# Recurrence projections in the mixer's first block, and transposes inside a block, in a hybrid encoder

## The chip, the cores and the metric

The kernel runs on one core of a Trainium2 chip. The metric is the device time of one execution in microseconds. The core has a matrix engine (TensorE, PE in the profile; its weight loads are PEld), a vector engine (VectorE, DVE), an activation engine (ScalarE, ACT), GpSimd (POOL) and a queue for loads (SyncE, SP).

## The reference

Two encoder layers over 256 tokens of width 1024, in float32. Each layer adds half a SwiGLU block, then a mixer, then half a SwiGLU block; a last norm follows.

```
x = x + 0.5 * swiglu(rms_norm(x, ffn1_norm), w_gate, w_up, w_down)
proj = rms_norm(x, mix_norm) @ w_in                     # 1024 -> 1792
xr, gate, q, k, v = split(proj, 512, 512, 512, 128, 128)
xc = depthwise_conv(xr, conv_w, width 4) + conv_b
r, i = sigmoid(xc @ w_a + b_a), sigmoid(xc @ w_x + b_x)  # 8 blocks, forward and backward
a = exp(-8 * softplus(-lam) * r); u = sqrt(1 - a*a) * (i * xc)
y_rec = gelu(gate) * (scan(a, u) + reverse scan(a', u'))
y_att = grouped attention(q, k, v, window, relative bias, sink)
x = x + concat(rms_norm(y_rec), rms_norm(y_att)) @ w_out
x = x + 0.5 * swiglu(rms_norm(x, ffn2_norm), ...)
```

## The kernel before

Tokens stand in two tiles of 128. Every product is made of three passes: activations and weights are each split into a high part (rounded) and a low part, and high x high, high x low and low x high are summed in PSUM. So each weight is loaded as raw float32 (`load_raw`, 1 MB pieces, three buffers, SyncE's queue), and `prep_one` makes a "half" of it: ScalarE copies the high part, VectorE subtracts it for the low part (for the halves in `VHI` VectorE does both). `prefetch` does that a few halves ahead; halves live in a ring of eight slots, except the mixer's first two, which use the tiles "w" and "i" (`EXTRA`).

There are eight PSUM banks in four pools of two: "a", "b", "g" and "c". `bank("gc")` takes "g" and "c" in turn, so that a bank comes back after four such allocations. "a" and "b" hold the output sums, the transposed tokens, and in the mixer attention's transposed probabilities ("b") and its output ("a").

The stages run one after the other. Between two of them stands `boundary` (L597): the stage before sums its last products (`tail`), residual updates, squares and norms of the two token tiles are put between them, `transposes(0)` turns the first tokens, and then `head(0)`, `transposes(1)` and `head(1)` of the stage that follows are issued. `transposes` (L534) makes eight transposes in TensorE and copies them into high (ScalarE) and low (VectorE) parts. TensorE, SyncE and GpSimd follow the order of the program; the order on ScalarE and VectorE is chosen by the planner when the kernel is built.

In a SwiGLU stage `head` (L699) multiplies one tile of tokens (stationary) by 512 columns, gate and up side by side: 3 passes of 8 matmuls. In the mixer `head` (L857) does so for the 256 columns of k and v only, both token tiles into one bank. The rest of the mixer follows a list, `ORDER` (L59). Each of its items is a letter and a number: x a recurrence projection (`xr`, L879: 24 matmuls of 256 columns, then the convolution `conv` on VectorE, read from PSUM), k the transposes of the keys (`head_end`, L872), q a query projection, l the gates of one quarter (`lru_gate`, L902: two banks, six matmuls each; ScalarE reads them with two activations a bank and makes two more), L the logits of two heads (two banks, read by VectorE, then exponentials on ScalarE), g a gate projection with its GELU, P, V and D the rest of attention, s a square root over all four quarters, c the scans, y their product with the gate, r, R, O and S the output projection.

Of the kernel before, what the change touches and what calls it, by code (L numbers as in the profile page):

```python
# [8 lines left out]
F32 = mybir.dt.float32  # L9
# [11 lines left out]
T = 256  # L21
# [34 lines left out]
CUT = 3  # L56
RCUT = 1
EARLY = 1
ORDER = "x0 k0 x1 q0 l0 q1 l1 L0 x2 L1 x3 g0 l2 P0 q2 l3 V0 P1 s0 L2 g1 c0 c1 q3 V1 P2 L3 c2 y0 g2 y1 V2 P3 g3 c3 V3 D0 y2 y3 r0 O0 r1 O1 r2 r3 R0 R1 R2 R3 S0".split()  # L59
HEAD = 2  # L60
VO = 6
VG = 1
# [5 lines left out]
def encoder_kernel(  # L68
# [56 lines left out]
    def bank(pool_):  # L125
        if pool_ == "gc":
            turn.append(turn.pop(0))
            pool_ = turn[0]
        return {"a": ps_a, "b": ps_b, "g": ps_g, "c": ps_c}[pool_].tile([128, 512], F32, tag=pool_, name="ps_" + pool_)
# [20 lines left out]
    def cols(w, c):  # L150
        return add_raw(w[:, c:c + 256].rearrange("(k p) c -> p k c", p=128), "kc")
# [7 lines left out]
    def head_half(name, r, j):  # L159
        add_half(name, [(r, j)], "kh")  # L160
# [26 lines left out]
        down(NM // 2 - 1)  # L187

    def plan_mix(st, wi, wo):
        r = cols(wi, 1536)  # L190
        for j in range(2):
            head_half((st, "kv", j), r, j)
        chunk = {}

        def chunk_of(n, p):
            if (n, p) not in chunk:
                chunk[n, p] = cols(wi, {"x": 0, "g": 512, "q": 1024}[n] + p * 256)
            return chunk[n, p]

        for n, i in ORDER:  # L200
            i = int(i)
            if n in "xg":
                col_half((st, {"x": "xr", "g": "gt"}[n], i), chunk_of(n, i // 2), i % 2)
            elif n == "q":
                add_half((st, "q", i), [(chunk_of("q", h), i * 64, h * 64, 64) for h in range(2)], "kc")
        for p in range(4):
            r = rows(wo, p * 256)
            for j in range(2):
                add_half((st, "o", 2 * p + j), [(r, j)], "rc")
# [118 lines left out]
    def W(*name):  # L328
        prefetch(index[name] + state["ahead"])
        return slot_t[name]  # L330
# [263 lines left out]
    def front():  # L594
        return tc.high_priority(offset=FRONT)

    def boundary(tail, evac, gi, head, ahead):  # L597
        prefetch(ahead)
        state["cap"] = ahead
        state["ahead"] = AHEAD  # L600
        tail(0, 0)
        with front():
            for hf in range(2):
                evac(0, hf)
                squares(0, hf)
            norm(0, gi)
        tail(1, 1)
        with front():
            evac(1, 0)
            transposes(0)  # L610
            squares(1, 0)
        tail(1, 2)
        with front():
            evac(1, 1)
            i1 = squares(1, 1)
            i2 = norm(1, gi)
        prefetch(ahead)
        state["behind"] = [i1, i2]
        state["cap"] = ahead + EARLY
        prefetch(ahead + FORCE)  # L620
        head(0)
        with front():
            state["behind"] = transposes(1)
        state["cap"] = 1 << 30
        prefetch(ahead + FORCE2)
        head(1)
        state["behind"] = []
        if gi % 3 != 1:
            load_gain(gi + 1)
# [61 lines left out]
    def ffn(st, acc_done):  # L691
# [4 lines left out]
        hn_t = {}  # L696
        late = {}

        def head(t):  # L699
            ps = bank("gc")  # L700
            ts_ = slice(t * 128, (t + 1) * 128)
            w = [W(st, "gu", q) for q in range(4)]
            for p in range(3):
                for k in range(KD):
                    x = cur["l" if p == 2 else "h"][:, k, ts_]
                    pe.matmul(ps, x, w[k // 2][p % 2][:, k % 2 * 512:k % 2 * 512 + 512],  # L706
                              start=(p == 0 and k == 0), stop=(p == 2 and k == KD - 1))
            hn_t[t] = gated(ps[:, 0:T], ps[:, T:2 * T])
            if t == 1:
                for q in range(4):  # L710
                    done((st, "gu", q))
# [126 lines left out]

    def mix(l):
        st = (l, 1)  # L840
        ps_x = {}
        xch_t, xcl_t = {}, {}
        xc_t, ge_t, a_t, yh_t, yl_t = {}, {}, {}, {}, {}
        q_t = mix_p.tile([128, NT, T], F32R, tag="q", name="q_t")
# [9 lines left out]
            done((st, name, i))  # L854
            return ps

        def head(t):  # L857
            if t == 0:
                ps_x["kv"] = bank("gc")
            ps = ps_x["kv"]  # L860
            natural([ps[:, t * 256:t * 256 + 256]], [[W(st, "kv", j) for j in range(2)]], t)
            if t == 1:
                for j in range(2):
                    done((st, "kv", j))
                new_tiles()
                act.activation(out=kv_t.rearrange("p t c -> p (t c)"), in_=ps, func=AF.Copy)

        def new_tiles():
            late["w"] = w_p.tile([128, 2 * NT, T], F32, tag="w", name="w_t")
            late["i"] = mix_p.tile([128, 2 * NT, T], F32, tag="i", name="i_t")  # L870

        def head_end():  # L872
            ps = bank("gc")
            for t in range(2):
                pe.transpose(ps[:, t * 128:(t + 1) * 128], kv_t[:, t, 0:128], eye_t)
            act.activation(out=k_t, in_=ps[:, 0:T], func=AF.Copy)
            dve.tensor_sub(out=kl_t, in0=ps[:, 0:T], in1=k_t.bitcast(F32))

        def xr(i):  # L879
            ps = unit("xr", i)  # L880
            with tc.high_priority(offset=MIXF):
                conv(i, ps)

# [333 lines left out]
```

## Time and profile before

| | |
|---|---|
| median of 3 runs | 938.35 us (937.91 to 938.55) |
| profiled execution | 938.13 us, of it span 936.4 us |
| PE busy | 926.0 us, 99% |
| PEld busy | 804.9 us, 86% |
| DVE busy | 696.8 us, 74% |
| ACT busy | 544.4 us, 58% |
| HBM read | 170.59 MB, 186 GB/s over the span |
| chain that ended last | PE 95%, DVE 2%, ACT 1%, issue 1%, DMA 1% |

Busy time of PE is modelled, since matmuls overlap: the distance from one start to the next tells the pace, and a gap between starts tells a wait. The shares are means over stages that are limited differently. The two mixers lie at about 197 to 286 us and 656 to 744 us; the granted clock is 1.00 in both.

### The profile page before, as it was taken

The numbers are of one execution on the slowest core, as the hardware profiler recorded it, in microseconds if no ns is written. First come the engines' busy times: TensorE is split into PE (matmuls) and PEld (weight loads), VectorE is DVE, ScalarE is ACT, GpSimd is POOL, SyncE is SP. The second block draws the span as 40 slices with busy tenths as digits, with TensorE's granted clock in tenths as the row PEclk, the third lists the DMA queues.
The fourth block names the chain that finished last, engine by engine and source line by source line (L and its number), as shares of the span: only waits on it lengthen the run. The fifth ranks groups of instructions, "written<-read, shape, count | busy, mean of one in ns | idle before, by whom it ended". The sixth has DMA issues, their size and how long they took to land.

```text
span 936.4 us, 13679 instructions
## 1 busy us (share of the span) xinstructions
PE 926.0 (99%) x5288; PEld 804.9 (86%) x5288; DVE 696.8 (74%) x1213; ACT 544.4 (58%) x1005; POOL 37.4 (4%) x60
## 2 busy tenths in 40 slices
PE   9999999999999999999999999999999999999997
PEld 8888888889988888888888888888999888888885
DVE  6888666769998876666688666666799887666663
ACT  7665555548855655555466555554687575555542
POOL 2300000000010000000030000000000100000000
PEclk9999999999999999999999999999999999999998
DMA  9786956714255755565557666555162576665521
GB/s 310 223 269 219 314 184 203 233 56 151 75 162 201 261 186 180 185 205 195 173 175 237 188 196 195 187 180 180 51 221 68 180 240 202 195 195 181 183 87 45
DMA packets 125009, 172.54 MB, mean 184 GB/s; under 512 B 3925, under 2 KB 108797, under 8 KB 124944
## 3 DMA queue, kind: packets, MB, share of 16 engines
q1 hardware_dynamic: 122192, 166.21, 54.8%
q0 software_dynamic: 2304, 4.87, 1.6%
q8 instruction: 41, 0.67, 0.3%
q10 hardware_dynamic: 448, 0.59, 0.2%
q14 instruction: 24, 0.20, 0.1%
HBM read 170.59 MB, written 3.16 MB: 186 GB/s over the span
## 4 chain that ended last, share of the span: by engine, by line
PE 95%; DVE 2%; ACT 1%; issue 1%; DMA 1%; POOL 0%; SPq 0%; POOLq 0%; DVEq 0%
PE ps_g L581 16%; PE ps_c L581 16%; PE ps_c L580 7%; PE ps_g L580 7%; PE ps_a L590 5%; PE ps_a L592 4%; PE ps_a L591 4%; PE ps_b L591 4%; PE ps_b L592 4%; PE ps_b L590 4%; PE ps_g L706 2%; PE ps_c L706 2%; PE ps_a L1021 1%; PE ps_g L569 1%; PE ps_g L570 1%; PE ps_g L571 1%
## 5 line engine op out<-in xcount | busy, mean ns | idle before, releaser
L308 DVE TENSOR_TENSOR wl<-raw,wh 128x1024 fp32r<-128x1024 f32 (+1 forms) x320 | 367.3, 1156 | 102.3 <-ACT wh L307 98.0
L307 ACT ACTIVATE wh<-raw 128x1024 fp32r<-128x1024 f32 (+1 forms) x306 | 301.9, 999 | 82.8 <-PE ps_b L592 60.5
L581 PE MATMUL ps_c<-xhl,wh 128*128 128x512 f32 x640 | 231.3, 396 | 0.0
L581 PE MATMUL ps_g<-xhl,wh 128*128 128x512 f32 x640 | 231.3, 396 | 0.0
L580 PE MATMUL ps_c<-xhl,wl 128*128 128x256 f32 x560 | 156.2, 279 | 0.0
L580 PE MATMUL ps_g<-xhl,wl 128*128 128x256 f32 x560 | 156.1, 279 | 0.0
L581 PEld LDWEIGHTS ps_c<-xhl,wh 128*128 128x128 f32 x640 | 120.1, 188 | 23.0
L581 PEld LDWEIGHTS ps_g<-xhl,wh 128*128 128x128 f32 x640 | 120.1, 188 | 23.0
L580 PEld LDWEIGHTS ps_c<-xhl,wl 128*128 128x128 f32 x560 | 105.6, 189 | 3.5
L580 PEld LDWEIGHTS ps_g<-xhl,wl 128*128 128x128 f32 x560 | 105.6, 188 | 3.5
L590 PE MATMUL ps_a<-wh,hh 128*128 128x512 f32 x168 | 65.7, 391 | 0.0
L590 PE MATMUL ps_b<-wh,hh 128*128 128x512 f32 x168 | 65.6, 391 | 0.0
L592 PE MATMUL ps_b<-wh,hl 128*128 128x512 f32 x168 | 65.4, 389 | 0.0
L591 PE MATMUL ps_b<-wl,hh 128*128 128x512 f32 x168 | 65.4, 389 | 0.0
L592 PE MATMUL ps_a<-wh,hl 128*128 128x512 f32 x168 | 65.4, 389 | 0.0
L591 PE MATMUL ps_a<-wl,hh 128*128 128x512 f32 x168 | 65.4, 389 | 0.0
L766 ACT ACTIVATE sg<-ps_g 128x256 f32<-128x256 f32 x40 | 15.4, 385 | 63.3 <-PE ps_g L581 63.3
L766 ACT ACTIVATE sg<-ps_c 128x256 f32<-128x256 f32 x40 | 15.3, 383 | 52.5 <-PE ps_c L581 51.6
L767 DVE TENSOR_TENSOR sg<-ps_g,sg 128x256 f32<-128x256 f32 x40 | 17.0, 425 | 32.8 <-ACT sg L766 32.7
L766 ACT ACTIVATE su<-ps_c 128x256 f32<-128x256 f32 x40 | 15.4, 386 | 39.0 <-PE ps_c L581 39.0
L754 ACT ACTIVATE hh<-th 128x256 fp32r<-128x256 f32 x80 | 33.4, 417 | 8.1 <-DVE th L748 7.8
L591 PEld LDWEIGHTS ps_a<-wl,hh 128*128 128x128 f32 x168 | 31.6, 188 | 6.9
(323 smaller groups left out, 1577.9 us busy)
## 6 DMA issues: line engine op xcount, KB each, us to landing
raw<-in_ffn_w_down_dram SPq DMA_DIRECT2D x44, 1024.0 KB, 5.0
raw<-in_ffn_w_gate_dram SPq DMA_DIRECT2D x43, 1024.0 KB, 5.4
raw<-in_ffn_w_up_dram SPq DMA_DIRECT2D x43, 1024.0 KB, 5.4
raw<-in_w_in_dram SPq DMA_DIRECT2D x14, 1024.0 KB, 5.5
raw<-in_w_out_dram SPq DMA_DIRECT2D x8, 1024.0 KB, 7.0
lb<-ld POOLq DMA_DIRECT2D x1, 2048.0 KB, 14.9
bias_t<-lb POOLq DMA_DIRECT2D x1, 1536.0 KB, 12.4
gain<-in_ffn_norm_dram SPq DMA_DIRECT2D x3, 512.0 KB, 4.6
```

The source lines that it names most:

```text
L307: act.activation(out=h3, in_=src, func=AF.Copy)
L308: dve.tensor_sub(out=l3, in0=src, in1=h3.bitcast(F32))
L569: pe.matmul(dst, wh[:, ks], xh[:, k, t0:t1], start=(k == 0), stop=False)
L580: pe.matmul(dst[:, 0:T], wl[:, ks], x2[:, 0, k, :], start=False, stop=False)
L581: pe.matmul(dst, wh[:, ks], x2[:, :, k, :], start=(k == 0), stop=(k == KD - 1))
L590: pe.matmul(acc[hf], ah[:, ts_], wh[:, cs], start=first, stop=False)
L591: pe.matmul(acc[hf], ah[:, ts_], wl[:, cs], start=False, stop=False)
L592: pe.matmul(acc[hf], al[:, ts_], wh[:, cs], start=False, stop=last)
L706: pe.matmul(ps, x, w[k // 2][p % 2][:, k % 2 * 512:k % 2 * 512 + 512], start=(p == 0 and k == 0), stop=(p == 2 and k == KD - 1))
L754: act.activation(out=hh, in_=src, func=AF.Copy)
L766: act.activation(out=s, in_=ps[:, T:2 * T], func=AF.Copy)
L767: dve.tensor_tensor(out=s, in0=ps[:, 0:T], in1=s, op=ALU.add)
```

## The change

The first block of the mixer gets the form of the SwiGLU stages' first block. Its four halves now hold k, v (256 columns) and the first two recurrence projections (256 columns) side by side; the first of them still use the tiles "w" and "i", the last two take the ring slots that the two projections' halves had. `head` makes 3 passes of 8 matmuls of 512 columns for each tile of tokens, into a bank of its own. ScalarE copies k and v of that tile into `kv_t`, and the 256 columns of the projections into `xn_x[t]`, in tiles that the SwiGLU stage uses. Since the block gives them with tokens on the partitions, `xr(0)` and `xr(1)` are no longer projections: two transposes each, into a bank of "a", from which the convolution reads. The transposes of the keys go to a bank of "b". In `boundary`, at all five boundaries, the second tokens' transposes and the prefetch behind them are issued within `head(0)`, ahead of its third pass. `ORDER` starts with q0, sets x2 behind q1, and moves l0, L1 and others accordingly.

```diff
--- before.py
+++ after.py
@@ -56,7 +56,7 @@
 CUT = 3
 RCUT = 1
 EARLY = 1
-ORDER = "x0 k0 x1 q0 l0 q1 l1 L0 x2 L1 x3 g0 l2 P0 q2 l3 V0 P1 s0 L2 g1 c0 c1 q3 V1 P2 L3 c2 y0 g2 y1 V2 P3 g3 c3 V3 D0 y2 y3 r0 O0 r1 O1 r2 r3 R0 R1 R2 R3 S0".split()
+ORDER = "q0 x0 k0 x1 q1 x2 l0 l1 L0 x3 L1 g0 l2 P0 q2 l3 V0 P1 s0 L2 g1 c0 c1 q3 V1 P2 L3 c2 y0 g2 y1 V2 P3 g3 c3 V3 D0 y2 y3 r0 O0 r1 O1 r2 r3 R0 R1 R2 R3 S0".split()
 HEAD = 2
 VO = 6
 VG = 1
@@ -187,10 +187,10 @@
         down(NM // 2 - 1)
 
     def plan_mix(st, wi, wo):
-        r = cols(wi, 1536)
-        for j in range(2):
-            head_half((st, "kv", j), r, j)
-        chunk = {}
+        chunk = {("x", 0): None}
+        r = cols(wi, 1536), cols(wi, 0)
+        for q in range(4):
+            add_half((st, "kv", q), [(r[0], q, 0), (r[1], q, 1)], "gu")
 
         def chunk_of(n, p):
             if (n, p) not in chunk:
@@ -199,6 +199,8 @@
 
         for n, i in ORDER:
             i = int(i)
+            if n == "x" and i < 2:
+                continue
             if n in "xg":
                 col_half((st, {"x": "xr", "g": "gt"}[n], i), chunk_of(n, i // 2), i % 2)
             elif n == "q":
@@ -618,11 +620,14 @@
         state["behind"] = [i1, i2]
         state["cap"] = ahead + EARLY
         prefetch(ahead + FORCE)
-        head(0)
-        with front():
-            state["behind"] = transposes(1)
-        state["cap"] = 1 << 30
-        prefetch(ahead + FORCE2)
+
+        def second():
+            with front():
+                state["behind"] = transposes(1)
+            state["cap"] = 1 << 30
+            prefetch(ahead + FORCE2)
+
+        head(0, second)
         head(1)
         state["behind"] = []
         if gi % 3 != 1:
@@ -696,11 +701,13 @@
         hn_t = {}
         late = {}
 
-        def head(t):
+        def head(t, between=None):
             ps = bank("gc")
             ts_ = slice(t * 128, (t + 1) * 128)
             w = [W(st, "gu", q) for q in range(4)]
             for p in range(3):
+                if p == 2 and between:
+                    between()
                 for k in range(KD):
                     x = cur["l" if p == 2 else "h"][:, k, ts_]
                     pe.matmul(ps, x, w[k // 2][p % 2][:, k % 2 * 512:k % 2 * 512 + 512],
@@ -838,7 +845,7 @@
 
     def mix(l):
         st = (l, 1)
-        ps_x = {}
+        ps_x, xn_x = {}, {}
         xch_t, xcl_t = {}, {}
         xc_t, ge_t, a_t, yh_t, yl_t = {}, {}, {}, {}, {}
         q_t = mix_p.tile([128, NT, T], F32R, tag="q", name="q_t")
@@ -854,30 +861,43 @@
             done((st, name, i))
             return ps
 
-        def head(t):
-            if t == 0:
-                ps_x["kv"] = bank("gc")
-            ps = ps_x["kv"]
-            natural([ps[:, t * 256:t * 256 + 256]], [[W(st, "kv", j) for j in range(2)]], t)
+        def head(t, between=None):
+            ps = bank("gc")
+            ts_ = slice(t * 128, (t + 1) * 128)
+            w = [W(st, "kv", q) for q in range(4)]
+            for p in range(3):
+                if p == 2 and between:
+                    between()
+                for k in range(KD):
+                    x = cur["l" if p == 2 else "h"][:, k, ts_]
+                    pe.matmul(ps, x, w[k // 2][p % 2][:, k % 2 * 512:k % 2 * 512 + 512],
+                              start=(p == 0 and k == 0), stop=(p == 2 and k == KD - 1))
+            act.activation(out=kv_t[:, t, :], in_=ps[:, 0:T], func=AF.Copy)
+            xn_x[t] = sum_p.tile([128, T], F32, tag=("sg", "su")[t], name="xn_x")
+            act.activation(out=xn_x[t], in_=ps[:, T:2 * T], func=AF.Copy)
             if t == 1:
-                for j in range(2):
-                    done((st, "kv", j))
+                for q in range(4):
+                    done((st, "kv", q))
                 new_tiles()
-                act.activation(out=kv_t.rearrange("p t c -> p (t c)"), in_=ps, func=AF.Copy)
 
         def new_tiles():
             late["w"] = w_p.tile([128, 2 * NT, T], F32, tag="w", name="w_t")
             late["i"] = mix_p.tile([128, 2 * NT, T], F32, tag="i", name="i_t")
 
         def head_end():
-            ps = bank("gc")
+            ps = bank("b")
             for t in range(2):
                 pe.transpose(ps[:, t * 128:(t + 1) * 128], kv_t[:, t, 0:128], eye_t)
             act.activation(out=k_t, in_=ps[:, 0:T], func=AF.Copy)
             dve.tensor_sub(out=kl_t, in0=ps[:, 0:T], in1=k_t.bitcast(F32))
 
         def xr(i):
-            ps = unit("xr", i)
+            if i < 2:
+                ps = bank("a")[:, 0:T]
+                for t in range(2):
+                    pe.transpose(ps[:, t * 128:(t + 1) * 128], xn_x[t][:, i * 128:(i + 1) * 128], eye_t)
+            else:
+                ps = unit("xr", i)
             with tc.high_priority(offset=MIXF):
                 conv(i, ps)
```

## Rows read from the trace of the kernel before

**Rows 1.** Windows, first mixer: stretch, us, busy of PE PEld DVE ACT POOL, clock, DMA

```profile
215.20:231.60 16.40, 16.36 (x140) 15.62 (x139) 15.69 (x41) 14.22 (x37) 0.00 (x0) 1.00 0.55 193
231.60:243.40 11.80, 11.80 (x106) 11.50 (x105) 11.61 (x23) 11.44 (x25) 0.00 (x0) 1.00 0.53 180
250.00:260.00 10.00, 10.00 (x87) 9.57 (x86) 10.00 (x33) 6.91 (x20) 0.00 (x0) 1.00 0.06 24
```

**Rows 2.** Timeline of TensorE, first mixer boundary: start, us, operation, count [idle before]

```profile
195.96 1.03 PE L544 MATMUL ps_a<-eye_t,xn 128*128 128x128 f32 x8
196.75 0.47 PE L590 MATMUL ps_b<-wh,hh 128*128 128x512 f32 x1
...
197.53 0.64 PE L561 MATMUL ps_c<-w_w,xhl 128*128 128x256 f32 x4
...
199.89 0.63 PE L561 MATMUL ps_c<-w_i,xhl 128*128 128x256 f32 x4
200.94 1.53 PE L544 MATMUL ps_b<-eye_t,xn 128*128 128x128 f32 x8 [0.42 <-DVE xn L526]
202.23 0.72 PE L561 MATMUL ps_c<-w_w,xhl 128*128 128x256 f32 x4
...
205.44 0.28 PE L569 MATMUL ps_g<-xhl,wh 128*128 128x256 f32 x1
```

**Rows 3.** Timeline of TensorE at the boundary between the two layers' SwiGLU blocks

```profile
471.18 1.98 PE L706 MATMUL ps_g<-wh,xhl 128*128 128x512 f32 x8
...
476.62 1.03 PE L544 MATMUL ps_b<-eye_t,xn 128*128 128x128 f32 x8
477.70 2.11 PE L706 MATMUL ps_c<-wh,xhl 128*128 128x512 f32 x8
...
481.46 1.98 PE L706 MATMUL ps_c<-wh,xhl 128*128 128x512 f32 x8
```

**Rows 4.** Timeline of VectorE: the second tokens' norm at those two boundaries

```profile
200.31 1.67 DVE L526 SCALAR_TENSOR_TENSOR xn<-x,rstd,gain 128x256 f32<-128x256 f32 x4 [0.66 <-POOL rstd L509]
...
473.96 1.67 DVE L526 SCALAR_TENSOR_TENSOR xn<-x,rstd,gain 128x256 f32<-128x256 f32 x4 [0.66 <-POOL rstd L509]
```

**Rows 5.** Timeline of TensorE, first mixer: gates l0, logits L1, gate projection

```profile
214.29 0.28 PE L911 MATMUL ps_g<-xch,gh_t 128*128 128x256 f32 x1
...
224.35 0.38 PE L976 MATMUL ps_g<-k_t,q_t 64*128 64x256 f32 x1
...
228.43 0.38 PE L569 MATMUL ps_c<-xhl,wh 128*128 128x256 f32 x1
```

**Rows 6.** Timeline of ScalarE: first and last operation of l0, first GELU square

```profile
215.21 0.48 ACT L919 ACTIVATE w_t<-ps_g,hba 128x256 f32<-128x256 f32 x1 [0.33 <-PE ps_g L913]
...
218.58 0.60 ACT L922 ACTIVATE w_t<-w_t,s_pos 128x256 f32<-128x256 f32 x1
...
231.61 0.39 ACT L940 ACTIVATE x<-ps_c 128x256 f32<-128x256 f32 x1 [0.25 <-PE ps_c L571]
```

**Rows 7.** Timeline of VectorE: first convolution begins, third begins and ends

```profile
208.52 0.55 DVE L888 TENSOR_SCALAR xc<-ps_g,par 128x256 f32<-128x256 f32 x1 [2.94 <-PE ps_g L571]
...
224.46 0.54 DVE L888 TENSOR_SCALAR xc<-ps_c,par 128x256 f32<-128x256 f32 x1
...
227.90 0.48 DVE L891 SCALAR_TENSOR_TENSOR xc<-ps_c,par,xc 128x255 f32<-128x255 f32 x1
```

**Rows 8.** Timeline of VectorE, then TensorE, at the fourth query and its logits

```profile
250.17 0.42 DVE L1116 SCALAR_TENSOR_TENSOR ql_t<-ps_g,q_t 128x256 fp32r<-128x256 f32 x1
250.64 0.38 PE L978 MATMUL ps_c<-k_t,ql_t 64*128 64x256 f32 x1
```

**Rows 9.** Timelines of SyncE's loads and of VectorE's residual update near the boundary

```profile
178.73 0.37 SPq L250 DMA_DIRECT2D raw<-in_w_in_dram  x1
183.13 0.37 SPq L250 DMA_DIRECT2D raw<-in_w_in_dram  x1
191.39 0.69 DVE L801 SCALAR_TENSOR_TENSOR x<-ps_a,x 128x512 f32<-128x512 f32 x1 [1.84 <-PE ps_a L592]
```

## The prediction

> **What bounds the kernel now.** I read the windows view over the attention block first, then the order of time of TensorE, ScalarE and VectorE, always asking which wait ends last there. In the mixer's attention block TensorE is busy without a break, and so, nearly, are VectorE and ScalarE [rows 1]: three engines share the bound, and VectorE is full for all of 250 to 260 us. That is what the reader should see: an edit that frees TensorE alone gains nothing further on unless the other two arrive earlier as well. At the change itself TensorE does wait. The first tokens' key/value block ends at 200.36, the second tokens' transposes wait for their normalised input and then the second block waits for the transposed copies: 202.23 before it goes on [rows 2]. The second layer repeats the pattern some 459 us later, so a net per mixer counts twice. The other three boundaries (before SwiGLU blocks) show less waiting [rows 3].
>
> **The change, part by part** (per mixer, first layer's clock).
>
> *Widening.* 48 key/value matmuls of 256 columns (20 in 2.36 us, 118 ns each [rows 2]) and the 48 of two recurrence projections (120 ns each: from 205.44 to 214.29 there are 72 such matmuls in 8.85 us, less 0.2 for two transposes [rows 2, 5]) become 48 of 512 columns at 227 ns (24 in 5.44 us [rows 3]). 5.66 + 5.76 - 10.88 = 0.5 us saved. A page of the Trainium skill speaks against even this: "TensorE: Matmul & The Clock Gate", section "Wait — 56ns, not 53.3ns?", gives a warm matmul its columns at 2.4 GHz and about 2.5 ns. By it 48 pairs would save an estimated 0.12 us, and the sum below would be 0.4 us worse per mixer. The trace differs, and its durations are used.
>
> *Added.* Four more 128x128 transposes, and all six now stand together: eight take 0.79 us [rows 2], so 0.6 + 0.1 for the change of kind, less 0.2 for the two that stood alone: 0.5 us lost. ScalarE gets four copies of 128x256 for one of 128x512, and eight weight pieces of 128x512 for four whole ones; VectorE the same pieces. These fall ahead of the convolutions, where VectorE waited 2.94 us for TensorE [rows 7] and ScalarE had as little to do; without that cover they would cost at most some 2 us of ScalarE, which joins the backlog below.
>
> *Moved transposes, mixer.* Before, 197.53 to 205.44 is 7.91 us for 5.66 of matmuls and 0.9 of transposes: 1.35 us of waiting [rows 2]. After, the transposes come up at 197.53 + 16 x 0.227 = 201.16. They cannot end before the second norm: it ends at 201.98 [rows 4], and TensorE went on 0.25 us behind it, so 202.23. That leaves 0.2 us of waiting; the eight matmuls behind (1.8 us) hide the copies of the transposed tokens. 1.1 us saved. What is queued behind the wait on TensorE is those eight matmuls; the prefetch (ScalarE, VectorE) that moves along is off the path.
>
> *Moved transposes, the other three boundaries.* Before: 471.18 to 483.27, 12.09 us [rows 3]. After: 3.63, then the transposes until 0.25 us behind the norm's end at 475.63 [rows 4], 475.88, then 0.1 + 1.8 + 5.4: 12.0 us. The wait for the copies is traded for a wait for the norm: 0 ± 0.1 us each.
>
> So TensorE alone would gain 0.5 - 0.5 + 1.1, about 1.15 us per mixer.
>
> *The new order.* Both gate blocks l0 and l1 now follow the third recurrence projection x2 without a projection between them, with logits L0 right behind. TensorE would reach l0 at 214.29 - 1.15 + 2 x 2.9 = 218.95. ScalarE's part of l0 begins 0.92 us after TensorE's [rows 5, 6], 219.87, and takes 3.6 us (215.21 to 219.1, less 0.3 of another operation [rows 6]). The four banks of the "gc" rotation return after four allocations. Counting through the new order, x3 reuses the first bank of l1, free only when ScalarE has done l0 and two operations of l1: 219.87 + 3.6 + 0.8 = 224.3 (0.5 less if an operation of l0 is passed over, 0.3 more if the copy of x2's convolution gets in between). By its own pace TensorE would be there at 223.2 (l0, l1 and L0 are the 10.06 us from 214.29 to 224.35 less two projections of 2.9 [rows 5]). So 0.6 to 1.4 of the 1.15 us is given back at once: the same work was done at 224.35 before. L1 moves behind x3.
>
> *ScalarE's backlog.* From 215.2 to 231.6 ScalarE did 14.22 us of work [rows 1], l0 first and the exponentials of L1 last; from 231.61 to the square root at 243.4 it works practically without idle time (11.44 of 11.8 us [rows 1, 6]). After, that work begins 4.66 us later. 0.6 us of it (a copy of q, one of a convolution) is done ahead, so it ends at 219.87 + 13.6 = 233.5 if nothing is left out, or at 231.6 if the two prefetch copies in it (1.9 us) are taken elsewhere. Against 231.6 that is 0 to 1.9 us late; I take one copy, 0.95 us, and give 0.55 back for the idle time that the chain had. The square root feeds the last scans, and behind it there is no room: the fourth query's low part ended at 250.59, and the matmul that reads it began at 250.64 [rows 8]. So I carry it through: **+0.4 us per mixer**, between -0.6 and +1.3. The lower end is a gain, since nothing excludes that both copies are out of the way.
>
> *Sum.* 938.13 (profiled execution, 936.4 span and 1.73 around it) + 2 x 0.4 + 3 x 0 = **938.9 us**. The profiled execution lies 0.2 us under the median of the runs, 938.35, with which it will be compared.
>
> **Rivals.** *TensorE's gain stays.* ScalarE fits its prefetch copies in while TensorE is at q1 and x2, where it has little to do, and works l1 off early. For it: two projections leave the rotation, so their convolutions hold no "gc" bank (before, the gate projection's start at 228.43 stands right behind the last step, at 228.38, of a convolution whose bank it takes [rows 5, 7]). Against it: [rows 1]. 938.13 - 2 x 1.15 = 935.8. A rule of the Trainium skill stands for this one: "Perfetto Trace Analysis", section "Matmul Optimizations", wants all eight PSUM banks used so that engines overlap, which here would mean that the convolutions read attention's idle banks while the rotation goes on.
>
> *The convolution holds l1's second bank, and the tail gets later.* x2's result now lies in the bank that l1's second half takes, four allocations on. Before, its convolution let go 4.1 us behind the matmuls (224.46 to 228.38, with other work in between [rows 7]); l1's second half wants the bank 2.2 us behind. If that spacing stays, TensorE stops for 1.9 us and ScalarE idles between as it did before (1.3 us). 0.95 + 1.3 - 0.25 = 2.0 us per mixer: 942.1. It decides from the point where x2's four convolution steps need over 2.2 us. For it: VectorE was never free there; against: its prefetch work can run ahead from 206 to 212 us, and then four bare steps take about 1.7 us.
>
> *A later load.* The split of the first chunk and the second chunk's now end together, so the second query chunk's load moves from 178.73 to about 183.13, when the next load's buffer came free [rows 9]. Four weight pieces behind it stand in ScalarE's and VectorE's order near the first tokens' residual updates. VectorE has 1.84 us of room there [rows 9], so 0 to 2.6 us per mixer reaches the first norm. At 1.2: 941.3.
>
> *The moved transposes do not do what they should.* If the norm came earlier by chance of the new order, all three other boundaries would save their 0.4 us: 937.7. If not, they save nothing, as in the sum.
>
> **How the numbers follow.** Forecast 0.46; gain stays 0.24; convolution holds the bank 0.18; later load 0.07; boundaries gain 0.05. The likeliest case alone spans 937.0 to 940.7 (-0.6 and +1.3 twice). To leave out no more than 2 in 10 the range goes from 935.7 to 942.0: half of the first rival lies about its lower end, and over a third of the second beyond its upper one. A measurement of this kernel can tell 0.2% from no change, about 1.9 us, so the borders are 936.5 and 940.2. Faster: most of the first rival and a trace of the forecast, 0.21. Slower: the second and third rival and the forecast's upper end, 0.29. Within: 0.50.
>
> **What would show it.** In the changed profile: 512-column matmuls of the mixer's first block at 227 ns and the second block starting without a gap (right); the first block's transposes at about 201.2 and their last pair waiting for the norm (right); TensorE waiting before x3, released by ScalarE's gate activations (right), or before l1's second half, released by a convolution step (second rival), or not at all with x3 at 223.2 (first rival). ScalarE should reach the square root 11.4 us behind the gate projection's square, 0.4 us later than before relative to the block's start. It is wrong if the two mixers differ from each other, if ScalarE is idle for over 2 us between l0 and the square root, or if the first norm of the mixer's boundary starts late.

## The result: 10.4 us slower, and the profile after

The changed kernel takes 948.71 us (median of 4 runs, 948.26 to 949.8) against 938.29 us (937.91 to 938.55): a ratio of 1.0112 (1.0100 to 1.0125). The forecast was 938.9 us, with 942.0 us as the upper end. The profiled execution took 948.88 us, its span is 947.1 us. TensorE's starts at the stage borders tell where the time went (us; the marks are the first transposes of a boundary, the transposes of a SwiGLU stage's first block's results, and the last matmul):

| stretch | before | after | longer by |
|---|---|---|---|
| start to the first mixer's boundary | 195.96 | 195.97 | 0.0 |
| first mixer | 195.96 to 284.47 | 195.97 to 289.65 | 5.2 |
| boundary behind it | to 303.73 | to 309.01 | 0.1 |
| SwiGLU stage | to 469.61 | to 474.92 | 0.0 |
| boundary between the layers | to 488.87 | to 494.16 | 0.0 |
| second layer's first SwiGLU stage | to 654.76 | to 661.68 | 1.6 |
| second mixer | to 743.26 | to 753.88 | 3.7 |
| boundary and last stage | to 929.11 | to 939.86 | 0.1 |

TensorE, first mixer, timeline of the changed kernel (answers to [rows 2] and [rows 5]):

```profile
197.54 0.63 PE L873 MATMUL ps_c<-w_w,xhl 128*128 128x512 f32 x2
...
201.25 1.23 PE L546 MATMUL ps_b<-eye_t,xn 128*128 128x128 f32 x8
202.24 0.71 PE L873 MATMUL ps_c<-w_w,xhl 128*128 128x512 f32 x2
...
209.71 0.28 PE L571 MATMUL ps_c<-xhl,wh 128*128 128x256 f32 x1
...
218.99 0.28 PE L931 MATMUL ps_g<-xch,gh_t 128*128 128x256 f32 x1
...
221.96 0.38 PE L931 MATMUL ps_g<-xch,gh_t 128*128 128x256 f32 x1 [1.37 <-ACT xch L919]
...
224.93 0.38 PE L996 MATMUL ps_c<-k_t,q_t 64*128 64x256 f32 x1 [0.38 <-DVE xc L911]
...
225.83 0.39 PE L571 MATMUL ps_g<-xhl,wh 128*128 128x256 f32 x1
...
229.82 0.39 PE L571 MATMUL ps_c<-xhl,wh 128*128 128x256 f32 x1
...
233.33 0.39 PE L931 MATMUL ps_g<-xch,gh_t 128*128 128x256 f32 x1 [0.38 <-DVE xc L911]
...
253.75 0.38 PE L998 MATMUL ps_c<-k_t,ql_t 64*128 64x256 f32 x1 [1.01 <-DVE ql_t L1136]
...
255.24 0.39 PE L571 MATMUL ps_c<-xhl,wh 128*128 128x256 f32 x1 [0.52 <-DVE ge L963]
```

Up to l0 at 218.99 everything is where the prediction had it (218.95). Then l1 (221.96) waits for its input, the second convolution; L0's second bank (224.93) and l2 (233.33) wait for the last step of a convolution, the third and the fourth; x3 starts at 225.83, the gate projection at 229.82. L3 waits at 253.75, and the gate projection behind it at 255.24.

VectorE, same kernel (answers to [rows 7] and [rows 8]), then ScalarE (answers to [rows 6]):

```profile
204.36 1.22 DVE L310 TENSOR_TENSOR wl<-raw,wh 128x1024 fp32r<-128x1024 f32 x1
210.88 0.69 DVE L307 CAST wh<-raw 128x1024 fp32r<-128x1024 f32 x1 [5.29 <-DMA raw<-in_w_in_dram]
211.61 2.43 DVE L310 TENSOR_TENSOR wl<-raw,wh 128x1024 fp32r<-128x1024 f32 x3
213.96 0.42 DVE L1136 SCALAR_TENSOR_TENSOR ql_t<-ps_c,q_t 128x256 fp32r<-128x256 f32 x1
214.29 0.54 DVE L908 TENSOR_SCALAR xc<-ps_a,par 128x256 f32<-128x256 f32 x1
...
218.64 0.55 DVE L908 TENSOR_SCALAR xc<-ps_a,par 128x256 f32<-128x256 f32 x1
...
253.28 0.42 DVE L1136 SCALAR_TENSOR_TENSOR ql_t<-ps_g,q_t 128x256 fp32r<-128x256 f32 x1
```

```profile
219.91 0.47 ACT L939 ACTIVATE w_t<-ps_g,hba 128x256 f32<-128x256 f32 x1 [1.66 <-PE ps_g L933]
...
221.49 0.42 ACT L919 ACTIVATE xch<-xc 128x256 fp32r<-128x256 f32 x1
...
246.10 1.92 ACT L1145 ACTIVATE w_t<-w_t 128x2048 f32<-128x2048 f32 x1
```

VectorE has nothing to do for 5.29 us ahead of 210.88 where it had 2.94 us [rows 7]: the planner put the cast of a gate weight first, and its load has not landed. Three subtractions of weights and a query's low part follow, so the first convolution begins at 214.29 (208.52 before) although its input was in PSUM at about 213.0, and the second one begins at 218.64. So of the 5.8 us by which the first convolution is later, some 4.5 us lie in when TensorE delivers its input, and 1.3 us in the work queued ahead of it. ScalarE's first gate activation comes at 219.91 (215.21), the square root at 246.10 (243.41).

The windows view from the second tokens' transposes to that square root (columns as in [rows 1]), of the changed kernel and then of the kernel before:

```profile
201.00:246.10 45.10, 42.89 (x328) 39.52 (x327) 37.97 (x88) 32.88 (x79) 0.00 (x0) 1.00 0.42 141
```

```profile
201.00:243.41 42.41, 42.32 (x356) 40.61 (x357) 38.41 (x84) 32.75 (x76) 0.00 (x0) 1.00 0.44 150
```

VectorE and ScalarE have the same work (38.0 and 38.4, 32.9 and 32.8 us). What grew is idle time: VectorE's from 4.00 to 7.13 us, ScalarE's from 9.66 to 12.22 us, TensorE's from 0.09 to 2.21 us. Of VectorE's 3.13 us, 2.35 stand ahead of the cast at 210.88.

Behind the square root nothing is made up. The chain of work that ended last (us from the start, duration, what ran) goes over VectorE alone until TensorE's gate projection:

```profile
248.56 1.20 DVE i_t L951 x2
249.76 0.60 DVE i_t L953
250.37 0.58 DVE i_t L955
...
253.36 0.33 DVE ql_t L1136
...
254.87 0.32 DVE ge L963
255.24 0.39 PE ps_c L571
```

The fourth query's low part is 3.11 us later than before (253.28 against 250.17 [rows 8]), and TensorE waits for it. The last step of the GELU (`ge`), whose end the gate projection waits for, begins at 254.79, 3.69 us later than in the kernel before, where one scan fewer stood ahead of it on VectorE:

```profile
251.10 0.40 DVE L943 SCALAR_TENSOR_TENSOR ge<-x,ps_c 128x256 f32<-128x256 f32 x1
```

Then, in the first mixer only, the granted clock falls (windows view, first and second mixer):

```profile
252.20:255.20 3.00, 1.51 (x13) 1.06 (x12) 3.00 (x8) 1.22 (x3) 0.00 (x0) 1.00 0.00 0
255.20:259.40 4.20, 4.16 (x22) 4.16 (x23) 4.20 (x16) 2.48 (x9) 0.00 (x0) 0.59 0.02 6
717.95:720.95 3.00, 1.48 (x13) 1.06 (x12) 3.00 (x8) 1.20 (x3) 0.00 (x0) 1.00 0.00 0
720.95:725.15 4.20, 4.18 (x36) 4.18 (x36) 4.20 (x16) 2.97 (x11) 0.00 (x0) 1.00 0.02 4
```

Both mixers have the same wait; after the first one TensorE got 22 matmuls done in 4.2 us, after the second one 36. That is the difference between 5.2 and 3.7 us.

The other place that lost time is the second layer's first SwiGLU stage. ScalarE, then TensorE, timelines of the changed kernel:

```profile
489.24 0.63 ACT L380 ACTIVATE gh_t<-gw 128x512 fp32r<-128x512 f32 x1 [2.94 <-DMA gw<-in_lru_w_x_dram]
...
496.16 1.06 ACT L309 ACTIVATE wh<-raw 128x1024 fp32r<-128x1024 f32 x1 [1.43 <-DMA raw<-in_ffn_w_down_dram]
497.13 0.36 ACT L773 ACTIVATE su<-ps_c 128x256 f32<-128x256 f32 x1
```

```profile
504.52 0.47 PE L583 MATMUL ps_g<-xhl,wh 128*128 128x512 f32 x1 [1.37 <-DVE hl L762]
```

ScalarE's queue has copies that wait for loads (2.94 and 1.43 us) ahead of the stage's first sums, and TensorE waits 1.37 us in the end, for a low part from VectorE.

### The profile page after: what moved, and what is told of

Its sections match the earlier page's. It is cut to its first block, busy times and chain, and to the rows that moved or that the text cites. A ratio compares the mean times of both kernels' runs of the same rounds, so it can differ in the third digit from the quotient of the medians.

```text
span 947.1 us, 13528 instructions
## 1 busy us (share of the span) xinstructions
PE 929.0 (98%) x5200; PEld 802.6 (85%) x5200; DVE 695.7 (73%) x1221; ACT 545.8 (58%) x1019; POOL 37.5 (4%) x60
## 4 chain that ended last, share of the span: by engine, by line
PE 89%; DVE 5%; issue 2%; ACT 1%; DMA 1%; POOL 1%; POOLq 0%; DVEq 0%; ACTq 0%
PE ps_g L583 15%; PE ps_c L583 15%; PE ps_g L582 7%; PE ps_c L582 7%; PE ps_a L592 4%; PE ps_a L594 4%; PE ps_a L593 4%; PE ps_b L594 4%; PE ps_b L593 4%; PE ps_b L592 4%; PE ps_c L873 1%; PE ps_g L873 1%; PE ps_c L713 1%; PE ps_g L713 1%; PE ps_a L1041 1%
## 5 line engine op out<-in xcount | busy, mean ns | idle before, releaser
L774 DVE TENSOR_TENSOR sg<-ps_g,sg 128x256 f32<-128x256 f32 x40 | 17.0, 425 | 32.8 <-ACT sg L773 32.7
```

The source lines that it names most:

```text
L774: dve.tensor_tensor(out=s, in0=ps[:, 0:T], in1=s, op=ALU.add)
```

## The experiments

Theories in turn: **A**, the loss lies in the mixer's new order, where VectorE's cast and subtractions ahead of the convolutions hold l1. **R**, the prediction's own: ScalarE's backlog holds the banks. **S**, the start of ScalarE's gate work sets the square root. **V**, VectorE's time lost ahead of its first convolution is not made up. For the SwiGLU stage (FFN in the expectations): **B** and **G2**, the moved transposes put weight copies ahead of the stage's first sums in ScalarE's queue; **G**, the split of the gate weights, which waits for its load there, does so by itself. "Mixer loss" is the lengthening between the marks of the table, first and second mixer; "(clock)" says that the granted clock fell in it.

**The move alone** (e1_move): the kernel before with the move at all five boundaries, in the mixer's old, narrow block too (cut):

```diff
-        head(0)
-        with front():
-            state["behind"] = transposes(1)
...
+        head(0, second)
```

> The kernel before with one part of the change alone: the second tokens' transposes issued ahead of the last third of the first tokens' block at all five boundaries; the mixer keeps its narrow first block and its old order. Theory A (the loss sits in the mixer's new order): the move by itself gives what the prediction's step on the moved transposes took, 1.1 us in each mixer and nothing at the three other boundaries, 938.1 - 2.2 = 935.9 us. Theory B (the loss of 1.76 us in the FFN behind the fourth boundary comes from the move, through ScalarE's changed order): 935.9 + 1.8 = 937.7 us.

Measured: 945.12 us, 1.0075 (1.006 to 1.009). Both theories fall. In the narrow block the transposes wait for the norm wherever they stand (1.35 us at 200.99), and the third pass now comes behind them: x0 starts at 206.11, 0.67 us later than before. The first mixer loses 2.6 us, 1.9 of it up to the first transposes of probabilities; TensorE waits 1.07 us at 230.34 for a convolution. The second mixer loses 1.5 us. The SwiGLU stage loses 3.6 us, its wait followed by a lower clock.

**The wide block and the order alone** (e2_widen):

```diff
-        head(0, second)
+        head(0)
+        second()
```

> The changed kernel without the moved transposes: the wide first block and the new order alone, the second tokens' transposes behind the whole first block as before. Theory A (l1 waits because VectorE has a cast that waits for its load, and three subtractions, queued ahead of the first convolution): in this kernel's order the three subtractions stand behind that convolution, and TensorE comes to l0 some 1.1 us later, so l1's wait of 1.65 us goes and with it most of what follows: 938 to 942 us. Theory R (the prediction's own: ScalarE's backlog behind the four gate steps in a row holds the banks): the order on TensorE is the same, so the loss stays and 1.1 us for each mixer comes on top: 948.7 + 2.2 = 951 us.

Measured: 948.86 us, 1.0118 (1.0101 to 1.0135); mixer loss 5.3 and 5.4 us (clock in both), nothing in the SwiGLU stage. q0 starts at 209.94, with the move at 209.71: the move is worth 0.23 us. l1 still waits (1.00 us), so A does not hold in this form; R had 951 us, more than was lost.

**Weight work held behind the second convolution** (e3_hold; `late["conv"]` is that convolution's last step; cut):

```diff
+                if n + i == "x1":
+                    state["behind"] = [late["conv"]]
+                if n + i == "l1":
+                    state["behind"] = []
```

> The changed kernel with one edit: the weight work that is queued from x1 to l1 is ordered on VectorE behind the second convolution's last step, so that no cast waits for its load ahead of the convolutions. TensorE's order and all its work stay. Theory A (VectorE's order): l1's wait of 1.65 us goes in both mixers, and the later waits that follow from it shrink: between 948.7 - 3.3 = 945.4 and 948.7 - 7.4 = 941.3 us. Theory R (ScalarE's backlog): l1's start moves, its successors wait for the banks as long as before: 948 to 949 us.

Measured: 948.06 us, 1.0105 (1.009 to 1.012). VectorE of this kernel, timeline:

```profile
212.68 0.54 DVE L908 TENSOR_SCALAR xc<-ps_a,par 128x256 f32<-128x256 f32 x1 [7.44 <-PE ps_a L898]
```

The cast is gone from ahead of the convolution, which begins 1.3 us earlier (this run stands 0.34 us ahead from its start on), and of l1's wait for it 0.55 us are left, for the low part. But VectorE now idles 7.44 us, and TensorE has other waits: 0.39 us at l1 for ScalarE, 1.33 us at L0's second bank for x2's convolution; mixer loss 4.2 us in both (clock in both). The fall of the clock is part of the 4.2 us, and how large a part is not known here; the loss without it may be under 3.7 us. The wait for the load is not the whole cause.

**L0 ahead of l1** (e4_L0first):

```diff
-ORDER = "q0 x0 k0 x1 q1 x2 l0 l1 L0 x3 ...
+ORDER = "q0 x0 k0 x1 q1 x2 l0 L0 l1 x3 ...
```

> The changed kernel with L0 ahead of l1 in the mixer's order, nothing else. Theory A (l1 waits for the second convolution, which is late on VectorE): L0, some 1.5 us of TensorE's work that needs only q0 and k0, covers most of l1's 1.65 us: 948.7 - 2.6 = 946.1 us; what comes later (VectorE's late chain) stays. Theory R (ScalarE's backlog): l1's gate work now comes still later on ScalarE, nothing is won: 948.7 us or up to 1 us more.

Measured: 952.87 us, 1.0152 (1.0137 to 1.0167), worse than either theory had it: mixer loss 7.2 and 6.3 us (clock in both). In the second mixer L0's second bank waits 1.67 us for ScalarE, the fourth query 1.42 us for VectorE.

**The old order** (e5_oldorder):

```diff
-ORDER = "q0 x0 k0 x1 q1 x2 l0 l1 L0 x3 L1 g0 ...
+ORDER = "x0 k0 x1 q0 l0 q1 l1 L0 x2 L1 x3 g0 ...
```

> The changed kernel with the order of the kernel before (x0 k0 x1 q0 l0 q1 l1 L0 x2 L1 x3 ...): the wide first block and the moved transposes stay, and l0 comes one and a half projections earlier. Theory S (the gate work of ScalarE and VectorE, 26 to 28 us from the first gate activation to the square root in either kernel and nearly without gaps, is what the mixer waits for; the change lets it begin at 219.9 where it began at 215.2): the first gate activation comes at 215.5 to 216.5, and the mixer's loss shrinks from 5.2 and 3.7 us to 1 us or less each; with the 1.8 us in the second layer's first FFN left, 939 to 943 us. Theory A alone (VectorE's cast ahead of the convolutions is the cause, wherever l0 stands): the cast is still ahead, 946 us or more.

Measured: 946.78 us, 1.009 (1.0073 to 1.0107); mixer loss 3.0 and 4.4 us (clock in the second). The cast, waiting for its load, still stands first on VectorE, the first convolution begins at 211.6, the first gate activation comes at 217.42 and the square root at 245.72, 28.3 us behind it (28.2 before). S had the distance right and the start wrong. The time is the one that A had (946 us or more), but the first convolution's input was in PSUM at about 211.0, so the cast held it for some 0.6 us only.

**x2 between l0 and l1** (e6_x2between), on top of the held weight work:

```diff
-ORDER = "q0 x0 k0 x1 q1 x2 l0 l1 L0 x3 ...
+ORDER = "q0 x0 k0 x1 q1 l0 x2 l1 L0 x3 ...
```

> The kernel of the run with the held weight work, with x2 moved from ahead of l0 to between l0 and l1, nothing else. Theory S (when the gate work begins decides): the first gate activation moves from 219.6 to 216.7, and as much as 2.9 us of each mixer comes back, less what the stretch has to spare: 948.1 - 4 to 6 = 942 to 944 us. Rival (the banks: four gate and logit steps bunched on TensorE wait for ScalarE's reads in any order): under 1 us in each mixer, 946 to 948 us.

Measured: 950.47 us, 1.0136 (1.0121 to 1.0151). Counted from the same start, the first gate activation does come earlier (217.38 instead of 219.92), the square root does not (248.99 instead of 247.46): S falls as the sole rule. Mixer loss 6.2 and 6.4 us (clock in both). L0's second bank waits 2.74 us for ScalarE.

**Gate-weight splits later** (e7_split, three steps of the stage later in the program, second layer; cut):

```diff
-                if st[1] == 0 and GSPLIT <= m < GSPLIT + 4:
+                if st[1] == 0 and GSPLIT + 3 * st[0] <= m < GSPLIT + 4 + 3 * st[0]:
```

> The changed kernel with the second layer's gate-weight splits three steps of the FFN later, nothing else. Theory G (TensorE's wait of 1.5 us at 502.8 comes from ScalarE, which has a gate-weight split queued ahead of the FFN's weight work and waits 2.9 us there for that split's load): the wait at 502.8 goes, 948.7 - 1.7 = 947.0 us. Rival (the FFN's own loads are late there, the split only fills the time): the wait stays, 948.7 us.

Measured: 948.79 us, 1.011 (1.0095 to 1.0125). It did not do what it was for: the planner left the split where it was, ScalarE waits 3.39 us for it at 488.67. The stage loses 1.3 us. Its mixers lose 3.7 and 3.7 us, without a fall of the clock.

**Old order, held weight work, later splits** (e8_oldhold, the edits of e5_oldorder, e3_hold and e7_split together):

> The changed kernel with three edits: the old order, the weight work held on VectorE behind the second convolution, and the second layer's gate-weight splits three steps later. Theory S with G: the first gate activation at about 214.5 (215.2 before the change), no wait in the second layer's first FFN, so no loss against the kernel before and up to 0.7 us won in each mixer: 937 to 939 us. If 941 us or more, a further loss is not yet named.

Measured: 957.99 us, 1.0212 (1.0196 to 1.0227), the slowest of all; mixer loss 8.2 and 7.4 us. The first gate activation comes at 215.43, as before the change, the square root at 245.59. The weight work that was held back (VectorE 32.7 us busy up to the square root instead of 38.0) comes later instead: the fourth query's low part lets TensorE wait 1.90 us, and stretches behind it wait for VectorE too.

**Splits queued 100 us later** (e9_gates, second layer; cut):

```diff
+                        if st[0] == 1:
+                            behind.enter_context(tc.issue_after(late["hh"].ins))
+                        split_gates(st[0], *divmod(m - GSPLIT, 2))
```

> The changed kernel with the second layer's four gate-weight splits queued on ScalarE behind the activations of the FFN's steps 12 to 15, some 100 us later; the earlier try moved them in the program but not in ScalarE's queue. Theory G (ScalarE's wait of 2.9 us for the gate weights' load, ahead of the FFN's weight work, makes TensorE wait 1.5 us at 502.8): that wait goes, 948.7 - 1.7 = 947.0 us. Rival (the FFN's own loads are late there): the wait stays, 948.7 us.

Measured: 949.18 us, 1.0111 (1.0094 to 1.0128). The splits are gone from ScalarE there, and the stage still loses 1.0 us; the mixers lose 5.2 us each (clock in both). ScalarE of this kernel:

```profile
496.38 1.06 ACT L309 ACTIVATE wh<-raw 128x1024 fp32r<-128x1024 f32 x1 [2.73 <-DMA raw<-in_ffn_w_down_dram]
497.35 0.36 ACT L773 ACTIVATE su<-ps_c 128x256 f32<-128x256 f32 x1
```

and of the kernel without the move (e2_widen), at the same place:

```profile
494.37 0.38 ACT L774 ACTIVATE su<-ps_c 128x256 f32<-128x256 f32 x1 [0.57 <-PE ps_c L583]
...
495.78 2.01 ACT L309 ACTIVATE wh<-raw 128x1024 fp32r<-128x1024 f32 x2 [0.72 <-DMA raw<-in_ffn_w_down_dram]
```

With the move a weight copy that waits for its load stands ahead of the stage's sum; without it, behind. The split is one such copy, not the only one.

**Less VectorE work, and its control** (e10_conv on the changed kernel, e11_convb on the kernel before): three of four convolution steps left out (cut).

```diff
             dve.tensor_scalar(o, ps, w(2), b, ALU.mult, ALU.add)
-            for j, d, n in ((0, 2, T - 2), (1, 1, T - 1)):
...
-            dve.scalar_tensor_tensor(out=o[:, 0:T - 1], in0=ps[:, 1:T], scalar=w(3), in1=o[:, 0:T - 1],
...
```

> The changed kernel with three of the four steps of each convolution left out (its output is not the reference's): some 4.9 us less VectorE work in each mixer, ahead of the square root; TensorE's and ScalarE's work as it was. Theory V (the wide block leaves VectorE without work for 5.3 us where it had 2.9 us without, in a stretch in which it is 90% busy and can't make that up): the mixers' loss of 5.2 and 3.7 us goes for the most part, 948.7 - 6 to 9 = 940 to 943 us. Theory S (ScalarE, 24.9 us of work from 219.9 to the square root): the square root stays where it is, 947 us or more.

> The kernel before with the same three steps of each convolution left out, as the control. All theories: TensorE is busy without gaps there (42.32 of 42.41 us up to the square root), so VectorE's 4.9 us less win next to nothing: 937 to 938.5 us. If it is 936 us or less, VectorE already held the kernel before in other places.

Measured: 942.50 us, 1.0052 (1.0031 to 1.0073), and 939.14 us, 1.001 (1.000 to 1.0019). The control gains nothing, as foreseen (it even loses 0.4 us per mixer, with a wait of 0.88 us for the fourth query). The changed kernel gains 6.2 us. Windows view of e10_conv, up to its square root:

```profile
201.00:244.05 43.05, 42.23 (x328) 39.39 (x327) 34.22 (x77) 32.60 (x79) 0.00 (x0) 1.00 0.43 148
```

TensorE idles 0.82 us there instead of 2.21, and the first mixer loses 1.2 us (the second 2.7, clock). The profiled execution took 946.1 us; its SwiGLU stage lost 3.8 us (clock). Its first convolution still begins late, at 214.23: less work on VectorE gives most of the first mixer's loss back. Shorter convolutions also bring l1's input sooner, so this alone does not separate VectorE's load from one late result; e3_hold, where that result came earlier and TensorE waited at L0's second bank instead, speaks for the load without proving it.

**Less ScalarE work** (e12_act): exponential and second tanh of both directions in one instruction each (cut; the exponential, the tanh likewise).

```diff
-                act.activation(out=a, in_=w, func=AF.Exp, scale=s_neg[:, c, pc:pc + 1], bias=s_neg[:, c, pc:pc + 1])
...
+            act.activation(out=a_t[c], in_=w2, func=AF.Exp, scale=s_neg[:, c, pc:pc + 1], bias=s_neg[:, c, pc:pc + 1])
```

> The changed kernel with the last two gate activations of both directions done by one instruction each, with the first direction's constants (its output is not the reference's): some 0.55 us less ScalarE work for each of a mixer's four gates, 2.2 us in a mixer. Theory S (ScalarE's work from the first gate activation sets the square root): 2 us come back in each mixer, 948.7 - 4 = 944.5 us. Theory V (VectorE's lost time): 947.5 to 949 us.

Measured: 946.84 us, 1.0101 (1.008 to 1.0123), between the two. The second mixer loses 2.2 us instead of 3.7, the first one 4.6 (clock, behind a wait of 1.95 us at l1, which the second has too). ScalarE is part of the bound as well; how the loss divides between the two engines stays open, since the planner lays out both queues anew with every edit.

**The lateness alone** (e13_qfirst), in the kernel before:

```diff
-ORDER = "x0 k0 x1 q0 l0 q1 l1 ...
+ORDER = "q0 x0 k0 x1 l0 q1 l1 ...
```

> The kernel before with q0 ahead of x0, k0 and x1 in the mixer's order, nothing else: the same TensorE work, l0 in the same place, only the first convolution comes one projection (2.9 us) later to VectorE. Theory V (VectorE's time lost ahead of its first convolution is not made up): a loss of 2 to 3 us in each mixer, as in the changed kernel with the old order, where the first convolution began equally late: 942 to 944.5 us. Rival (the loss needs the wide block; here only l0 can wait, 1 us or less): 938.2 to 940.2 us.

Measured: 946.54 us, 1.0091 (1.0074 to 1.0108): more than V had, 4.3 and 3.9 us per mixer (clock in the first). VectorE, timeline, and the windows up to the square root in the first and second mixer:

```profile
208.96 0.42 DVE L1116 SCALAR_TENSOR_TENSOR ql_t<-ps_g,q_t 128x256 fp32r<-128x256 f32 x1 [3.35 <-ACT q_t L1115]
211.02 0.70 DVE L305 CAST wh<-raw 128x1024 fp32r<-128x1024 f32 x1 [1.64 <-DMA raw<-in_w_in_dram]
211.63 0.54 DVE L888 TENSOR_SCALAR xc<-ps_c,par 128x256 f32<-128x256 f32 x1
```

```profile
201.00:247.00 46.00, 44.11 (x356) 42.00 (x357) 38.27 (x87) 32.73 (x77) 0.00 (x0) 0.96 0.40 138
664.04:709.63 45.59, 43.17 (x356) 40.65 (x357) 38.24 (x87) 32.61 (x76) 0.00 (x0) 1.00 0.41 139
```

No wide block, no moved transposes, the same 38.3 us of VectorE work: its first convolution comes 3.1 us later, TensorE waits 1.44 us for it at l0, and the square root comes 3.6 us later. In the second mixer, at a clock of 1.00, the two are 3.0 and 3.1 us later, and 3.9 us are lost. So a later first convolution, with what the planner then makes of the queues, is enough for a loss of this size. It does not set the size: 0.7 us later cost 2.6 and 1.5 us (e1_move), 3.1 us later cost 3.0 us (e5_oldorder, first mixer, clock of 1.00), and 5.8 us later 3.7 us (the changed kernel).

**The move in the mixers only** (e14_ffnold), **and with the old order** (e16_mixmove):

```diff
-        head(0, second)
+        if gi % 3 == 1:
+            head(0, second)
+        else:
+            head(0)
+            second()
```

> The changed kernel with the second tokens' transposes back behind the whole first block at the three FFN boundaries, and ahead of its last third in the two mixers as changed. Theory G2 (the move at the FFN boundary puts weight copies, which wait for their loads, ahead of the FFN's first sums in ScalarE's queue): no wait near 502.8, the mixers as in the changed kernel: 948.7 - 1.7 = 947.0 us. Rival (the mixers' move or the lateness of the whole kernel makes that wait): 948.7 us.

> The same with the old order of the mixer as well: the mixers should lose what they lost with the old order alone (3.0 and 3.7 to 4.4 us), the FFN nothing: 946.8 - 1.1 = 945.7 us by Theory G2. It is the best version that the runs so far point to; none of the theories has it under 938.2 us.

Measured: 946.14 us, 1.0089 (1.0074 to 1.0104), and 945.61 us, 1.0083 (1.0068 to 1.0098), both near the times expected. G2 holds: the SwiGLU stage loses nothing. The profiled execution of e16_mixmove took 947.07 us; its mixers lose 4.7 and 4.3 us (clock in both), the first more than was expected. The mixers of e14_ffnold lose 3.68 and 3.71 us, the clock falls in neither (its window at the place shown above):

```profile
252.20:255.20 3.00, 1.50 (x13) 1.06 (x12) 3.00 (x8) 1.21 (x3) 0.00 (x0) 1.00 0.00 0
255.20:259.40 4.20, 4.16 (x36) 4.16 (x36) 4.20 (x16) 2.95 (x11) 0.00 (x0) 1.00 0.02 6
```

That gives the ledger: 2 x 3.7 for the mixers, 1.6 for the SwiGLU stage, 5.2 - 3.7 = 1.5 for the clock, 0.2 at two boundaries: 10.7 us, the difference of the spans. No version came under the kernel before. A fourth load buffer, which might let the gate weight land before 210.9, was not tried.

## Why the prediction was wrong

The step that failed is the one on ScalarE's backlog: it gave +0.4 us per mixer, and the mixers lost 5.2 and 3.7 us. Ahead of it failed the cover that the step on the added work relied on. The steps in their order:

**Widening and moved transposes: the sum right, the parts not.** 1.15 us were to come free on TensorE up to l0, and l0 came at 218.99 for 218.95, partly by luck. The wait at the second tokens' transposes did go, but the move gives 0.23 of the 1.1 us that it was given (e2_widen): the wide block itself, 24 matmuls in 5.57 us, covers the norm. And those matmuls come at 232 ns, not 227, so the widening by itself saves 11.42 - 11.14 = 0.3 us. The Trainium skill's figure ("TensorE: Matmul & The Clock Gate", "Wait — 56ns, not 53.3ns?", about 216 ns for 512 columns by its rule) is further off here than in the trace of before.

**The other three boundaries: right.** 0 ± 0.1 us each; 0.1, 0.0 and 0.1 measured. But what the prediction said of the prefetch that moves along, that it "is off the path", fails one stage behind a boundary: in the second layer's first SwiGLU stage the copies stand in another order, and the stage loses 1.6 us, a term that the sum did not have. e14_ffnold, without the move there, takes that loss away; with the splits gone 1.0 us of it stays (e9_gates). That it is the copies waiting for loads that carry the rest is read from the order of ScalarE's queue and was not tested by itself.

**Added: the cover was not there.** The step hid the added copies in time in which VectorE "waited 2.94 us for TensorE". It did not ask what VectorE could do in that time once its first input comes later: nothing, since the weights were not loaded either. The 2.94 us became 5.29, and behind them three subtractions stood ahead of the first convolution.

**The new order: a wait that was not on the list.** x3 was to wait for ScalarE until 224.3; it started at 225.83, because l1 ahead of it waited for its own input and L0's second bank for x2's convolution. ScalarE's last read of l1's first bank ended at 224.64, near the 224.3, and no longer mattered. The step counted through the banks and never asked when the second convolution would end (221.2), behind a first one that began 5.8 us later.

**ScalarE's backlog: the mechanism right, the size not.** "Behind it there is no room" held: what the square root was late by went through to the end of the mixer. But it was late by 2.69 us, not 0.4. The step took ScalarE's work as the measure: of the 4.66 us by which it begins later, it was to get back 2.7 us as idle time (16.40 - 14.22 and 0.55) and 1.55 us as work done elsewhere (0.6 and 0.95). From the first gate activation to the square root it got back 1.3 and 0.7 us (windows view, the changed kernel, then the kernel before):

```profile
219.91:246.10 26.19, 23.98 (x202) 22.34 (x201) 24.39 (x63) 24.94 (x61) 0.00 (x0) 1.00 0.52 181
215.21:243.41 28.20, 28.16 (x244) 27.13 (x243) 27.30 (x63) 25.66 (x62) 0.00 (x0) 1.00 0.54 187
```

ScalarE is idle for 1.25 us there, less than the 2 us that the prediction named as a sign against it, so there it is as full as the step had it; its longest wait is for VectorE (1.00 us at 232.52). The work of both engines up to the square root did stay the same; it began later (first convolution by 5.8 us, first gate activation by 4.7), and VectorE, 91% busy up to the square root before, got only part of that back. Behind the square root came 0.4 us more of weight work ahead of the fourth query and a scan of 0.6 us ahead of the GELU's last step: 2.7 + 0.4 + 0.6 = 3.7 us in either mixer. The clock, for which the sum had no term, adds 1.5 us in the first; so the two mixers differ, which the prediction had named as a sign of being wrong.

**The rivals.** The nearest was the second (a convolution holds a bank, the tail gets later; 942.1). It had the bank wrong: l1's second half began at 223.12 without a wait, while x2's convolution read its bank until 224.87. The wait for that convolution is at L0's second bank, six allocations behind x2 and not the four after which a bank was said to come back, and another such wait is at l2; they are 0.38 us each instead of 1.9 us, and the tail is late for another reason. TensorE's gain did not stay; the later load came (183.30) and showed no effect, the first tokens' transposes stood at 195.97; the other boundaries gained nothing. The opening sentence of the prediction was the one to follow to its end: three engines share the bound, so an edit that lets TensorE do more before the other two get their first input takes from them what it gives to TensorE.

## What to carry to other kernels

Where several engines are nearly full in one stage, look first at when each of them gets its first input, not at how much work it has: joining products into one wider block delivers all of them at its end, and the engines behind it stand still until then. An order that is moved by one step on TensorE is laid out anew by a planner on the other engines; look there for instructions that wait for a load and for what is queued behind them, also one stage further on. If nothing behind has room, 0.67 us of lateness can come with a loss of 2.6 us, as in e1_move's first mixer.

## What the hardware showed

TensorE's granted clock fell at waits that look harmless: 0.59 over 255.20 to 259.40 (most of it at 1.2 GHz), after TensorE had been busy for 1.51 of 3.00 us. The step from one 256-column matmul to the next was 0.21 us there instead of 0.12. The same wait in the second mixer, and in both mixers of e14_ffnold, left the clock at 1.00. So a wait of about 1.5 us can cost another 1.5, or not. The changed kernel's runs spread over 1.5 us where those of the kernel before spread over 0.6; that the clock makes this spread was not shown.
